# A GELU-gate kernel: the first two tiles loaded and stored in two pieces each, and the last tile computed in steps of 1, 1, 2 and 4 rows

## The chip, the cores and the metric

One core of one Trainium2 chip. The metric is the device time of one execution in microseconds (us). Times are medians of a kernel's runs.

## The reference

```python
def reference(x):                       # x: (32, 512, 2048) float32
    half_dim = x.shape[-1] // 2
    x1, x2 = x[..., :half_dim], x[..., half_dim:]
    gelu_x1 = 0.5 * x1 * (1 + erf(x1 / np.sqrt(2)))
    return (gelu_x1 * x2).astype(np.float32)   # (32, 512, 1024)
```

There are 16384 rows of 8 KB in (134.2 MB) and 4 KB out (67.1 MB).

## The kernel before

A tile is 128 partitions x 8 rows: 8.39 MB in, 4.19 MB out, 16 tiles. There are two input buffers and two output buffers. SyncE issues all loads, ScalarE issues the stores of tiles 0 to 13.

```python
    R, STEP = 8, 4
    x_t = x_flat.rearrange("(n p r) d -> n p r d", p=P, r=R)
    o_t = out_flat.rearrange("(n p r) d -> n p r d", p=P, r=R)
    ... # xpool and opool, two buffers each; load(i) fills one x_tile on SyncE
    ahead = [load(0), load(1)]
    for i in range(n_tiles):
        x_tile = ahead.pop(0)
        o_tile = opool.tile([P, R, half], out.dtype, name="o_tile")
        last = i == n_tiles - 1
        for r in range(0, R, STEP):
            rows = slice(r, r + STEP)
            nc.scalar.activation(out=x_tile[:, rows, :half], in_=x_tile[:, rows, :half], func=GELU)
            nc.vector.tensor_mul(out=o_tile[:, rows, :], in0=x_tile[:, rows, :half], in1=x_tile[:, rows, half:])
            if last:
                store(nc.sync, i, o_tile, rows)
        if not last:
            store(nc.sync if i == n_tiles - 2 else nc.scalar, i, o_tile, slice(0, R))
        if i + 2 < n_tiles:
            ahead.append(load(i + 2))
```

In memory the 8 rows of one partition lie in one piece, so a whole tile moves as runs of 64 KB (load) and 32 KB (store), half a tile as runs of 32 KB and 16 KB. The trace has one packet record for each run: in the kernel before, 2048 of 64 KB for the 16 loads of 128 partitions.

## Time and profile before

| | before |
|---|---|
| time, 3 runs | 471.6 us (471.57 to 472.48) |
| span of the profiled run | 469.7 us |
| VectorE, ScalarE busy | 30%, 25% |
| DMA engines busy | 99.5% |
| bytes over the span | 429 GB/s |

A packet record has queue, size, start and duration of one run. A completion record is the 4-byte write that ends a transfer, one for each of the 16 engines (528 in the kernel before, for its 33 transfers); a transfer has landed when the last of its 16 is there. The records do not name the engine; where I speak of single engines I have chained each packet to the one that starts as it ends. That attribution is rough where several engines run close together. By these chains a completion takes a turn of its queue: on one engine of before a load packet starts at 66.59, a store's completion at 69.02 and the next load packet at 69.03, with no store packet between.

### The profile page before, as it was taken

What the parts mean: (1) busy time and instruction counts of PE and PEld (TensorE: products, weight loads), DVE (VectorE), ACT (ScalarE), POOL (GpSimd) and SP (SyncE); (2) the same over time, 40 slices, a digit from 0 to 9 for tenths busy, and PEclk for the clock granted to TensorE, in tenths of its full rate; (3) what the DMA queues carried; (4) which work ended last, traced back from release to release, by engine and by line L of the source; (5) the groups of instructions that cost most, each with busy time, mean ns of one, the idle gap of its engine ahead of it and who ended that gap; (6) DMA issues with size and microseconds to landing.
All of it is one profiled execution on the core that took longest, in us unless ns stands there. A gap on an engine that the chain in (4) does not pass through costs nothing.

```text
span 469.7 us, 213 instructions
## 1 busy us (share of the span) xinstructions
DVE 140.2 (30%) x32; ACT 115.2 (25%) x33; POOL 0.2 (0%) x4
## 2 busy tenths in 40 slices
DVE  0070704307042070520606115060250702507043
ACT  1052306023060320603206041060500505005060
POOL 0000000000000000000000000000000000000000
DMA  8999999999999999999999999999999999999988
GB/s 357 446 446 357 446 446 446 402 446 458 391 446 444 433 463 402 435 413 491 402 419 430 491 402 402 446 491 402 402 446 480 413 402 444 449 446 402 474 375 357
DMA packets 4754, 201.35 MB, mean 429 GB/s; under 512 B 528, under 2 KB 528, under 8 KB 528
## 3 DMA queue, kind: packets, MB, share of 16 engines
q1 hardware_dynamic: 2736, 142.61, 70.5%
q10 hardware_dynamic: 2016, 58.72, 29.0%
q14 instruction: 2, 0.02, 0.0%
HBM read 134.22 MB, written 67.11 MB: 429 GB/s over the span
## 4 chain that ended last, share of the span: by engine, by line
DMA 77%; DVE 14%; ACT 6%; DVEq 1%; issue 0%; SPq 0%; ACTq 0%
DMA x_tile<-in_x_dram 77%; DVE o_tile L57 14%; ACT x_tile L54 6%; DVEq L93 1%; SPq L41 0%; ACTq L54 0%
## 5 line engine op out<-in xcount | busy, mean ns | idle before, releaser
L57 DVE TENSOR_TENSOR o_tile<-x_tile 128x4096 f32<-128x4096 f32 x32 | 140.2, 4422 | 321.6 <-ACT x_tile L54 321.6
L54 ACT ACTIVATE x_tile<-x_tile 128x4096 f32<-128x4096 f32 x32 | 114.0, 3608 | 340.5 <-DMA x_tile<-in_x_dram 340.5
L54 ACT ACT_TABLE_LOAD x1 | 1.3, 1283 | 0.7 <-PEq L82 0.7
L82 POOL MEMSET const-bfloat16-1.0<- 128x1 bf16 x1 | 0.1, 102 | 0.0
L82 POOL MEMSET const-uint8-127<- 128x1 uint8 x1 | 0.1, 101 | 0.0
L82 POOL MEMSET const-float32-0.0<- 128x1 f32 x1 | 0.1, 99 | 0.2 <-issue 0.2
L82 POOL MEMSET const-float32-1.0<- 128x1 f32 x1 | 0.1, 98 | 0.0
## 6 DMA issues: line engine op xcount, KB each, us to landing
out_dram<-o_tile ACTq DMA_DIRECT2D x14, 4096.0 KB, 41.8
out_dram<-o_tile SPq DMA_DIRECT2D x1, 4096.0 KB, 24.8
out_dram<-o_tile SPq DMA_DIRECT2D x2, 2048.0 KB, 6.9
x_tile<-in_x_dram SPq DMA_DIRECT2D x16, 45.5
```

The source lines that it names most:

```text
L54: nc.scalar.activation(out=x_tile[:, rows, :half], in_=x_tile[:, rows, :half], func=GELU)
L57: nc.vector.tensor_mul(out=o_tile[:, rows, :], in0=x_tile[:, rows, :half], in1=x_tile[:, rows, half:],)
L82: nc = _bacc.Bacc("TRN2", target_bir_lowering=False, num_devices=1)
L93: with _tile.TileContext(nc) as tc:
```

## The change

The intent: start computing and storing when half a tile has landed, and make the first half of the last tile ready sooner by small steps.

```diff
-    R, STEP = 8, 4
+    R = 8
 ...
-    ahead = [load(0), load(1)]
+    def load_small(i):
+        x_tile = xpool.tile([P, R, dim], x.dtype, name="x_tile")
+        for h in range(2):
+            rows = slice(4 * h, 4 * h + 4)
+            nc.sync.dma_start(out=x_tile[:, rows, :], in_=x_t[i][:, rows, :])
+        return x_tile
+
+    ahead = [load_small(0), load_small(1)]
 ...
-        for r in range(0, R, STEP):
-            rows = slice(r, r + STEP)
+        for lo, hi in ((0, 1), (1, 2), (2, 4), (4, 8)) if last else ((0, 4), (4, 8)):
+            rows = slice(lo, hi)
 ...
-            if last:
-                store(nc.sync, i, o_tile, rows)
-        if not last:
+            if (last or i < 2) and hi % 4 == 0:
+                store(nc.sync if last else nc.scalar, i, o_tile, slice(hi - 4, hi))
+        if 2 <= i < n_tiles - 1:
             store(nc.sync if i == n_tiles - 2 else nc.scalar, i, o_tile, slice(0, R))
```

## The prediction

> **What bounds the kernel now.** I read the page first, engines and DMA rows together:
>
> ```profile
> span 469.7 us, 213 instructions
> DVE 140.2 (30%) x32; ACT 115.2 (25%) x33; POOL 0.2 (0%) x4
> ...
> DMA  8999999999999999999999999999999999999988
> ...
> q1 hardware_dynamic: 2736, 142.61, 70.5%
> q10 hardware_dynamic: 2016, 58.72, 29.0%
> ```
>
> No compute engine is busy a third of the time; the DMA engines are full in every slice (9 is 90% or more) but the first and the last two. q1 is the SyncE queue (all loads, the last three stores), q10 the ScalarE queue (14 stores): 70.5 + 29.0 = 99.5% of the 16 engines' time. Then the chain of waits, two rounds of it:
>
> ```profile
> 56.85 45.55 DMA x_tile<-in_x_dram
> ...
> 102.48 3.62 ACT x_tile L54
> 106.11 0.03 issue
> 106.13 8.77 DVE o_tile L57 x2
> 114.90 0.02 issue
> 114.92 45.50 DMA x_tile<-in_x_dram
> ```
>
> It reads as a loop: load lands, GELU 3.62, two multiplies 8.77, the buffer is free, next load 45.5. But 45.5 is not what a load costs alone. A round is 114.92 - 56.85 = 58.07 us for two tiles, in which 2 x (8.39 + 4.19) = 25.17 MB move: 433 GB/s. Load 0, alone on the engines, needed 22.67 - 0.73 = 21.9 us. So the 45.5 is queueing behind other transfers: a bandwidth limit that looks like a loop. Head and tail, from the timeline:
>
> ```profile
> 0.73 56.45 SPq L41 DMA_DIRECT2D x_tile<-in_x_dram  x4
> 22.67 7.12 ACT L54 ACTIVATE x_tile<-x_tile 128x4096 f32<-128x4096 f32 x2 [20.66 <-DMA x_tile<-in_x_dram]
> 26.32 8.76 DVE L57 TENSOR_TENSOR o_tile<-x_tile 128x4096 f32<-128x4096 f32 x2 [26.32 <-ACT x_tile L54]
> 35.11 0.38 ACTq L45 DMA_DIRECT2D out_dram<-o_tile  x1
> ```
>
> ```profile
> 434.51 27.63 SPq L45 DMA_DIRECT2D out_dram<-o_tile  x3
> 449.37 7.12 ACT L54 ACTIVATE x_tile<-x_tile 128x4096 f32<-128x4096 f32 x2 [20.18 <-DMA x_tile<-in_x_dram]
> 453.02 8.76 DVE L57 TENSOR_TENSOR o_tile<-x_tile 128x4096 f32<-128x4096 f32 x2 [18.54 <-ACT x_tile L54]
> ```
>
> Loads 0 and 1 start together, so the first store, at 35.11, finds load 1 still on the engines. At the end load 15 lands at 449.3, store 14 (waiting in the same queue since 434.5) follows, and the halves of store 15 are issued at 457.45 and 461.80. In the trace's packet records the first data packet starts at 1.74 and the last ends at 468.51. Store 14 ends at about 458.3 on nearly every engine and store 15 starts at 458.31 to 458.8: in the whole tail the engines are idle some 0.2 us. The only other hole is at the passage from load 1 to store 0, where the last 64 KB packet of each engine takes 3.1 to 3.8 us in place of 2.42 (about 1.1 us).
>
> [...]The packet records agree: in the steady state an engine alternates one 64 KB load packet (2.42 us) with one 32 KB store packet (1.21 us), eight of each for a tile, 8 x 3.63 = 29.0 us, which is half a round; a completion record takes a turn of its own.[...]
>
> **The change, part by part.**
> (1) Split loads. Two 8 MB loads become four 4 MB loads, two more issues at about 0.33 us each on SyncE, behind running transfers. Rows 0-3 of tile 0 land near 0.73 + 21.9/2 + about 1 = 12.7, not 22.67. GELU to 16.3, multiply to 20.7, first half store at 20.7 (before: 35.1); the second half and load 2 follow load 0's rest: 22.6 + 3.6 + 4.4 = 30.6 (before 35.1). On a full DMA this moves bytes about and removes none: gain 0.
> (2) Split stores. The same bytes in 16 KB packets, where I see 0.61 us each for store 15: the same rate. But turns go by packets: a 64 KB load packet beside a 16 KB store packet gives loads 4/5, not 2/3, and each half store spends a turn of its own on completion. Until store 1 is out, loads run ahead of stores.
> (3) An issue order. In the instruction order of the changed kernel, ScalarE issues both half stores of tile 1 after both its GELUs, so the first waits for load 1's second half, near 51, plus 3.6: about 55 (before, store 1 at 56.85; now its second half near 59). By hand, with turns: store 0 done near 52, then load 2 is alone until store 1's packets come in near 60 (new packets come two or so behind those already taken up, as store 0 did: issued 35.11, first packet 42.25). Load 2 has then done about 4 of its 8 packets unaccompanied; from there one for one, load 3 ends with some 3 packets of store 1b left. That backlog of 3 to 4 packets then persists, since the turns are one for one.
> (4) What the backlog does. The output buffer of tile i is that of tile i-2, whose store now ends about 3 x 3.63 + 2.42 + 0.3 = 13.6 us after load i, and GELU is done at +4. So from tile 3 on VectorE waits about 8 to 10 us for the store. It then ends at 13.6 + 8.8 = 22.4 after load i, and issues load i+2; load i+1 ends at 29.0. Still 6 us early, so the DMA stays full: cost 0 in the steady state.
> (5) The tail. The last load lands about 4 us earlier (445 for 449), because stores are behind by 3.5 packets x 1.21. Step sizes 1, 1, 2, 4: multiplies of 1024, 1024, 2048 and 4096 take[...] 1.22 + 1.22 + 2.29 + 4.42 = 9.15 us, against 8.84: two instructions more cost 0.3. Without a buffer wait the first half would be done at +6.3 after landing (GELUs of about 1.05, 1.05 and 1.9 us, an estimate from 3.61/4 and 3.61/2 with about 0.1 added, then 2.29), not +8.1; the second at 7.6 + 4.4 = +12.0, not +12.4. Gain on the path at most the 0.2 us hole. With the buffer wait the first multiply starts only when store 13 has landed: 3 x 2.42 + 1.21 + 0.3 = 8.8 after load 15; the first half is ready at 8.8 + 4.7 = 13.5 and moves from 14.4 (0.86 us from issue to first packet, as for store 15). Store 14 has by then 3 or 4 packets done and ends at about 3 x 2.42 + 5 x 1.21 = 13.3. A hole of 1.1 us, against 0.2 now.
> Sum: 0 + 0 + 0 + (1.1 - 0.2) = +0.9 us; 471.6 + 0.9 = 472.5, and I put the middle at 472.4.
>
> **The rivals.**
> A. No backlog: if transfers go in order of issue (the first half store waiting for all of load 1), the steady state is that of before, the tail hole closes: -0.2, 471.4. Store 0's delay from 35.11 to 42.25 could be read so; the strict alternation afterwards, with the completion taking its turn, speaks for turns and a short lookahead.
> B. The intended gain: a compute-bound tail, 1.8 us sooner for the first half, 0.4 for the second, and an earlier head: 469.5 to 471. Against it: the tail holds 8.39 MB after load 15, 8.39/0.433 = 19.4 us, and 449.3 + 19.4 = 468.7 is where the data ended. It could only come from the 1.1 us hole at the first store closing.
> C. A larger backlog, 4.5 packets: the next load is issued barely in time and the tail hole grows to some 2.4 us: 473.8. More such 1.1 us holes at each first store would land there too.
>
> **Range and chances.** [...]2% slower (481) would need 9 us of idle DMA, four times rival C. From A and B below and C above, with before's runs themselves at 471.57 to 472.48: 470.7 to 474.0. Faster 0.01, same 0.98, slower 0.01.
>
> **What would show it.** Right, if VectorE waits from tile 3 on are put down to the stores and no longer to the GELU, stores of 4 MB take longer to land than 41.8 us (near 48) and loads less than 45.5 (near 37), the last GELU starts at about 445, and data ends at 469 or a little over. Rival A: waits as before, last GELU at 449. Rival B: data ending before 467.5. The sum is wrong in kind if the DMA row shows a slice under 8 in the middle.

The sum: +0.9 us, 472.5. What is cut from step 5 is only how I came to the lengths of the small steps, which the trace of before does not have. The trace of the changed kernel has them: multiplies of 128x1024, 128x2048 and 128x4096 take 1222, 2285 and 4422 ns, GELUs 1048, 1893 and 3609. The four multiplies add up to 9.15 us, but from first start to last end they take 8.90, where the two of before take 8.76. In "halves of tile 0", below, which has these tail steps and no wait on a store, the halves of the last tile are done 6.1 and 11.8 us after its first GELU starts, in before 8.1 and 12.4. An estimate from the trace: at the 433 GB/s of the round above, 201.33 MB take 465.0 us, and 2% faster would be 462.2.

## More of the kernel before

The prediction shows the page's engine and DMA rows, the chain and both ends of the timeline. Two views it does not show matter later. First what VectorE waited for (columns: us in total, times, longest us):

```profile
DVE o_tile L57 <- ACT x_tile L54: 321.6, 16, 26.3
```

VectorE waits for the GELU and never for a store. Then the DMA issues (last column: median us from issue to landing):

```profile
out_dram<-o_tile ACTq DMA_DIRECT2D x14, 4096.0 KB, 41.8
...
x_tile<-in_x_dram SPq DMA_DIRECT2D x16, 45.5
```

## The result, and the profile after

475.75 us (475.08 to 479.37, 6 runs) against 471.54 (471.3 to 472.48, 6 runs): 4.2 us slower. The ratio is 1.0101, 95% interval 1.0069 to 1.0132. Ratios here are the mean time of one kernel's runs over that of the other's runs of the same rounds, so not quite the ratio of the medians. The runs of the changed kernel also scatter over 4.3 us; five of the six runs of before lie within 0.3 us.

The page of the changed kernel:

```profile
span 473.8 us, 223 instructions
...
DMA  8999999999999999999999999999999999999987
...
q1 hardware_dynamic: 3024, 142.61, 70.0%
q10 hardware_dynamic: 2304, 58.72, 28.7%
```

The DMA engines look as full as before, in every slice but the last. That row is a mean of 16 engines over 11.8 us, and what went wrong hides in it. What VectorE waited for:

```profile
DVE o_tile L65 <- DMA out_dram<-o_tile: 178.5, 9, 20.3
DVE o_tile L65 <- ACT x_tile L62: 145.1, 9, 21.2
```

In 9 tiles VectorE's wait is now ended by a store that has to free the output buffer. The 178.5 us are the whole idle time before those tiles, not what the stores add: that is the start of the multiply less the end of its GELU step, 2.6 us at tile 4, 0.4 at tile 10, 0.1 from tile 11 to 14 and 1.9 in the last tile. The DMA issues:

```profile
out_dram<-o_tile ACTq DMA_DIRECT2D x12, 4096.0 KB, 49.0
...
out_dram<-o_tile ACTq DMA_DIRECT2D x4, 2048.0 KB, 28.1
...
x_tile<-in_x_dram SPq DMA_DIRECT2D x14, 44.8
```

A whole-tile store lands after 49.0 us, not 41.8. Both are signs of the predicted lag of stores behind loads. The loads do not: 44.8, where I expected near 37. The timeline shows why, in three places (columns: start us, us, what, count, and in brackets the idle time before it and what ended that):

```profile
20.91 0.37 ACTq L46 DMA_DIRECT2D out_dram<-o_tile  x1
...
30.60 84.26 SPq L42 DMA_DIRECT2D x_tile<-in_x_dram  x4
...
51.71 8.46 ACTq L46 DMA_DIRECT2D out_dram<-o_tile  x2
...
128.55 7.12 ACT L62 ACTIVATE x_tile<-x_tile 128x4096 f32<-128x4096 f32 x2 [21.29 <-DMA x_tile<-in_x_dram]
134.72 8.76 DVE L65 TENSOR_TENSOR o_tile<-x_tile 128x4096 f32<-128x4096 f32 x2 [20.21 <-DMA out_dram<-o_tile]
...
334.40 7.12 ACT L62 ACTIVATE x_tile<-x_tile 128x4096 f32<-128x4096 f32 x2 [22.58 <-DMA x_tile<-in_x_dram]
...
452.23 7.31 ACT L62 ACTIVATE x_tile<-x_tile 128x1024 f32<-128x1024 f32 x4 [21.88 <-DMA x_tile<-in_x_dram]
455.17 8.90 DVE L65 TENSOR_TENSOR o_tile<-x_tile 128x1024 f32<-128x1024 f32 x4 [19.43 <-DMA out_dram<-o_tile]
```

The head is nearly as predicted: half stores issued at 20.9 and 30.6, load 2 at 30.6. Tile 1's first half store waits only until its second GELU has started (51.70) and is issued at 51.71, not at 55. At tile 4 the loads are ahead, GELU at 128.55 where before it starts at 131.71. By tile 11 the lead is gone (334.40; before, 334.52). The last GELU starts 2.9 us later than before (452.23, before 449.37), not 4 earlier. And the last multiplies wait for store 13 until 455.17.

The lead melted on a few engines only. Completions of load 15, in us: before, first 448.3, middle 448.5, last 448.9. After, first 445.5, middle 445.8, last 451.8. So most engines did finish 3 us sooner (the prediction said 4); the slowest came 6 us behind them. The gap between first and last completion grew from load to load: 1.5 us at load 4 (126.6 to 128.1), 3.2 at load 9 (271.6 to 274.8), 6.3 at load 15. Between 105 and 445 us the packet records of before hold one packet that takes over 0.05 us too long; those of the changed kernel hold 61, all of them 64 KB load packets, with 13.0 us too much in sum. By my chains of packets they sit on some five engines, once or twice a tile, 0.1 to 0.6 us each; the engine that came last had some 4 us more of it than before.

The tail by stretches (columns: stretch, length, busy time of VectorE, ScalarE and GpSimd, PE clock, DMA share, GB/s), before and after:

```profile
450.00:457.40 7.40, 4.38 (x2) 6.50 (x2) 0.00 (x0) 1.00 1.00 431
457.40:458.60 1.20, 1.20 (x2) 0.00 (x0) 0.00 (x0) 1.00 0.55 232
```

```profile
450.00:457.00 7.00, 1.83 (x2) 4.77 (x4) 0.00 (x0) 1.00 1.03 445
457.00:460.60 3.60, 3.60 (x3) 2.54 (x1) 0.00 (x0) 1.00 0.25 107
```

Bytes are booked by packet and the stretches are short, so these shares are rough; but the hole is plain: from about 457.8 to 460.5 most engines have nothing to do, because store 14 is out and the first half of tile 15 is not ready. By packet records the hole is 2.1 us on the mean of the engines, before 0.2. Completions of the very last store: before 468.1 to 468.5 on all 16; after, 470.4 to 470.6 on 14 engines and 471.9 and 472.4 on two. So of the 3.9 us by which the last data ends later (468.5 to 472.4), the hole accounts for about 2 and the late engines, the stragglers, for the rest.

The hole too comes of late engines. The last multiplies wait for store 13, which the middle engine finished at 450.6 and the last one at 454.2. Twelve of the 16 were done by 451.1. Had the others come with them, the multiplies could have started near 452, the half tile been ready 4.5 us later (its three multiplies run from 455.17 to 459.7) and its store moved 0.86 us after that (in before issued at 457.45, first packet at 458.31), at about 457.4, before the engines ran dry at 457.8: no hole. That is an estimate from these trace times, not a run.

### The profile page after: what moved, and what is told of

Its sections match the earlier page's. It is cut to its first block, busy times and chain, and to the rows that moved or that the text cites. A ratio compares the mean times of both kernels' runs of the same rounds, so it can differ in the third digit from the quotient of the medians.

```text
span 473.8 us, 223 instructions
## 1 busy us (share of the span) xinstructions
DVE 140.5 (30%) x34; ACT 115.7 (24%) x35; POOL 0.2 (0%) x4
## 4 chain that ended last, share of the span: by engine, by line
DMA 82%; DVE 13%; DVEq 1%; ACT 1%; issue 0%; SPq 0%
DMA out_dram<-o_tile 72%; DVE o_tile L65 13%; DMA x_tile<-in_x_dram 10%; DVEq L101 1%; ACT x_tile L62 1%; SPq L52 0%; DVEq L65 0%
## 5 line engine op out<-in xcount | busy, mean ns | idle before, releaser
L65 DVE TENSOR_TENSOR o_tile<-x_tile 128x4096 f32<-128x4096 f32 (+2 forms) x34 | 140.5, 4171 | 323.6 <-DMA out_dram<-o_tile 178.5
L62 ACT ACTIVATE x_tile<-x_tile 128x4096 f32<-128x4096 f32 (+2 forms) x34 | 114.4, 3408 | 343.2 <-DMA x_tile<-in_x_dram 343.2
## 6 DMA issues: line engine op xcount, KB each, us to landing
x_tile<-in_x_dram SPq DMA_DIRECT2D x14, 44.8
```

## The experiments

Eighteen kernels ran, all correct. The first four undo the change part by part, the next ones copy one suspected effect into the kernel before, the last ones cut the guilty part finer. Diffs are against the kernel named. "Slow packets" are those more than 0.05 us over the usual 2.42 (64 KB), 1.21 (32 KB) or 0.61 us (16 KB), between 105 and 445 us, a copy's own packets included where a run has copies; hole means idle engine time between the last load and the last store, on the mean of 16 engines. The waits are counted as the profile puts them down: tiles in which it names a store as what ended VectorE's wait. It can name the GELU where a store ended it, as "all lag stores" will show.

| run | time, us | before | waits of VectorE on stores | slow packets, us in sum | load 15: first / last completion | hole, us |
|---|---|---|---|---|---|---|
| changed kernel | 475.75 | 471.54 | 9 | 13.0 | 445.5 / 451.8 | 2.1 |
| loads only | 471.65 | 471.55 | 0 | 0.2 | 448.1 / 449.1 | 0.5 |
| stores only | 475.5 (its four fast runs) | 471.55 | (2) | (209) | (460.3 / 464.2) | (1.5) |
| tail only | 471.61 | 471.55 | 0 | 0.2 | 448.1 / 448.9 | 0.0 |
| head only | 476.41 | 471.55 | 9 | 9.4 | 445.5 / 451.3 | 2.3 |
| half shift of loads | 471.72 | 471.65 | 0 | 0.4 | 448.3 / 449.6 | 0.6 |
| all shift of loads | 472.04 | 471.65 | 0 | 0.3 | 448.4 / 449.1 | 0.2 |
| all lag stores | 472.67 | 471.65 | 2 (by the records 10) | 12.5 | 446.7 / 448.8 | 0.8 |
| half lag stores | 471.86 | 471.65 | 7 | 0.9 | 446.0 / 448.7 | 0.0 |
| half shift, fraction | 474.15 | 471.49 | 0 | 17.9 | 449.7 / 451.9 | 1.6 |
| half lag, fraction | 473.42 | 471.49 | 9 | 19.0 | 447.4 / 449.7 | 0.2 |
| matched halves | 472.06 | 471.49 | 0 | 7.0 | 448.3 / 450.0 | 0.1 |
| half turn offset | 472.94 | 471.61 | 0 | 4.6 | 448.7 / 450.3 | 0.8 |
| two small, control | 472.11 | 471.61 | 0 | 0.5 | 448.2 / 448.9 | 0.3 |
| lag in step | 481.32 | 471.61 | 1 | 129 | 453.1 / 458.8 | 2.0 |
| issue order | 476.02 | 471.61 | 10 | 5.1 | 445.5 / 450.6 | 1.5 |
| halves of tile 0 | 471.38 | 471.47 | 0 | 0.3 | 447.9 / 448.5 | 0.0 |
| halves of tile 1 | 474.88 | 471.47 | 7 | 5.5 | 445.7 / 453.1 | 3.3 |
| lag in mid-run | 474.16 | 471.47 | 1 | 8.7 | 448.5 / 451.8 | 2.3 |

The profiled run of "stores only" counts as slow (over 1.5% above the fastest of its kernel; its granted clock is 1.000 as in all runs here), so its values stand in brackets and nothing is built on them.

### Part by part

Loads only: the kernel before with `load_small` for tiles 0 and 1.

```diff
-    ahead = [load(0), load(1)]
+    ahead = [load_small(0), load_small(1)]
```

> Only the loads of tiles 0 and 1 are split; stores and tail as before. Theory (half stores of 16 KB packets lose their turns, stores fall behind, and engines drift apart): no half stores, so VectorE waits on the GELU only, the 4 MB stores land in about 42 us as before, all 16 engines stay within 1 us: 471.5 +- 0.7 us. Rival (split loads are what sets the engines out of step): 474 or more.

471.65 us, ratio 1.0001 (0.9989 to 1.0013). No waits on stores; the stores even land sooner (33.3 us). Split loads are harmless.

Stores only: the kernel before with the change's store lines.

```diff
-            if last:
-                store(nc.sync, i, o_tile, rows)
-        if not last:
+            if (last or i < 2) and hi % 4 == 0:
+                store(nc.sync if last else nc.scalar, i, o_tile, slice(hi - 4, hi))
+        if 2 <= i < n_tiles - 1:
```

> Only the stores of tiles 0 and 1 are split; loads and tail as before. Theory: the backlog appears, and larger than in the changed kernel because store 1's halves wait longer: VectorE waits on stores in most tiles, 4 MB stores land in 48 us or more, time 474 to 477. Rival (split loads): 471.5.

476.65 us over all six runs (475.43 to 486.64), two of them slow; the four fast ones have 475.43 to 477.73 and a ratio of 1.0093 (1.0073 to 1.0113). The half stores alone bring a loss as large as the changed kernel's.

Tail only: the kernel before with the change's steps in the last tile.

```diff
-        for r in range(0, R, STEP):
-            rows = slice(r, r + STEP)
+        for lo, hi in ((0, 1), (1, 2), (2, 4), (4, 8)) if last else ((0, 4), (4, 8)):
+            rows = slice(lo, hi)
 ...
-            if last:
-                store(nc.sync, i, o_tile, rows)
+            if last and hi % 4 == 0:
+                store(nc.sync, i, o_tile, slice(hi - 4, hi))
```

> Only the 1, 1, 2, 4 steps of the last tile. Theory: the first half store is issued 1.8 us earlier after the last load, the last one 0.4 us; it closes the 0.2 us hole: 471.3, within 0.5 us of before. Rival (the smaller steps cost at the end): 472.5 or more. Rival (compute-bound tail): 470 or less.

471.61 us, ratio 1.0002 (0.9988 to 1.0015). The hole of 0.2 us closes in its records and the time does not show it.

Head only: the changed kernel with the tail as before.

```diff
-        for lo, hi in ((0, 1), (1, 2), (2, 4), (4, 8)) if last else ((0, 4), (4, 8)):
+        for lo, hi in ((0, 4), (4, 8)):
```

> Split loads and stores in the head, the tail in steps of 4 as before. Theory: all of the loss is made in the head and the time is the changed kernel's, 475 to 476. Rival (tail): 471.5 to 472.5.

476.41 us, ratio 1.0105 (1.0087 to 1.0123): as the changed kernel, with 9 waits on stores and the same spread of completions.

What was open now was how half stores of two tiles cost 4 us at the other end of the run.

### Are engines that run out of step slow?

In the changed kernel four engines take up the first half store one load packet sooner than the rest (near 24.5 us instead of 26.1) and are out of step from then on. The next four runs put that, or the lag, into the kernel before by tiny copies from output tile 4 to a scratch tile. A copy of 8 partitions has 8 packets and 8 completions (half shift of loads: 4770 packets, 536 of them under 512 B, against 4754 and 528), so it runs on 8 engines only, where I count a turn for its data and one for its completion.

```diff
+        if i == 4:
+            for k in range(1):                                   # N copies
+                s_tile = spool.tile([8, 512], x.dtype, name=f"s_tile{k}")      # PARTS, WORDS
+                nc.sync.dma_start(out=s_tile, in_=o_tile[:8, 0, :512])          # QUEUE
         if not last:
             store(nc.sync if i == n_tiles - 2 else nc.scalar, i, o_tile, slice(0, R))
```

Half shift of loads: as shown, on SyncE.

> Before plus one 16 KB copy (8 partitions, output tile 4 to a scratch tile) on the SyncE queue: on 8 of the 16 DMA engines it takes two turns of the load queue, so these 8 run out of step with the other 8 from tile 4 on, with no backlog of stores. Theory D (engines out of step make load packets slow): 473.5 or more, 8 engines with stalls. Rival B (the backlog of stores makes them slow): 471.6 to 472, no stalls.

471.72 us, ratio 1.0000 (0.9988 to 1.0012). The engines are out of step in the packet records and slow packets do not come.

All shift of loads, the control: the same with 16 partitions.

```diff
-                s_tile = spool.tile([8, 512], ...);  in_=o_tile[:8, 0, :512]
+                s_tile = spool.tile([16, 512], ...); in_=o_tile[:16, 0, :512]
```

> Control: the same copy with 16 partitions, so all 16 engines lose the same two turns and stay in step. Both theories: 471.6 +- 0.5.

472.04 us, ratio 1.0011 (0.9999 to 1.0024).

All lag stores: two copies of 16 partitions on ScalarE.

```diff
-            for k in range(1):  ... [8, 512]  ... nc.sync.dma_start
+            for k in range(2):  ... [16, 512] ... nc.scalar.dma_start
```

> Before plus two 32 KB copies (16 partitions, output tile 4 to scratch) on the ScalarE queue ahead of store 4: every engine loses four turns of the store queue, about 14 us of lag of stores behind loads, in step and without any half store. VectorE should wait on stores from tile 6 on. Theory D: only the tail hole that the prediction worked out, 472.3 to 473. Rival B: 474.5 or more, with slow load packets.

472.67 us, ratio 1.0021 (1.0009 to 1.0033), in the range of theory D and below the rival's 474.5. All engines stop for about 0.7 us at the copies themselves, in two packets each, which is nearly all of the 12.5 us of slow packets (12.5 / 16 = 0.8). The profile puts only two of VectorE's waits down to stores. Its timeline from 210 to 262 us, at tile 7, shows that this count misleads:

```profile
216.96 7.12 ACT L56 ACTIVATE x_tile<-x_tile 128x4096 f32<-128x4096 f32 x2 [21.86 <-DMA x_tile<-in_x_dram]
224.26 8.76 DVE L59 TENSOR_TENSOR o_tile<-x_tile 128x4096 f32<-128x4096 f32 x2 [20.19 <-ACT x_tile L56]
```

The first GELU step ends at 220.57, and the multiply starts 3.7 us after it. In these 3.7 us store 5, which has to free the buffer, gets its last completion (223.66). The profile names the second GELU step, which happens to end at 224.08. In every tile from 6 to 14 the multiply starts 0.5 to 0.6 us after the last completion of the store two tiles back and 3.6 or 3.7 us after its GELU step; at tile 12 VectorE passed its wait at 369.40, before the second GELU step ended (369.51). So this is the lag that was asked for, on all engines and in step. It holds VectorE up longer than the changed kernel does (at most 2.6 us), only two slow packets follow the copies, and the price is 1.0 us (by the interval 0.4 to 1.6), of which the stop at the copies can be some 0.7.

Half lag stores: two copies of 8 partitions on ScalarE.

```diff
-            for k in range(1):  ... nc.sync.dma_start
+            for k in range(2):  ... nc.scalar.dma_start
```

> The same two copies with 8 partitions, so 8 engines lag by four turns of the store queue and 8 do not. Theory D: 475 or more, the changed kernel's loss or worse. Rival B: about that of the run in which all engines lag, since a store lands when its last engine is done.

471.86 us, ratio 1.0004 (0.9992 to 1.0016), against 475 or more that the theory wanted. Its waits of VectorE:

```profile
DVE o_tile L59 <- ACT x_tile L56: 179.1, 9, 26.2
DVE o_tile L59 <- DMA out_dram<-o_tile: 142.3, 7, 20.7
```

Here are nearly as many waits on stores as in the changed kernel (7 against 9, 4 MB stores at 49.1 us), on engines in two groups apart, and the 0.2 us that it costs are within the noise. But these waits are short: beyond the GELU step the store adds 0.2 to 0.9 us a tile. So it is the run before this one that shows long waits on stores to be cheap, and this one that being out of step by whole packets costs nothing measurable. My theory, that engines out of step have slow packets, fell.

### Out of step by a fraction?

The next guess: in the changed kernel the lagging engines' packets start 1.4 to 1.8 us off the others', a fraction of a 3.63 us turn. The copies' times in the next expectations are estimates from the 2.42 us of a 64 KB packet: 12 KB 0.45, 14 KB 0.53; the 1.4 us of the control below is 4 x 1.21 and 0.15 for 4 KB, less 3.63.

Half shift, fraction: the SyncE copy of 8 partitions with 14 KB a partition.

```diff
-                s_tile = spool.tile([8, 512], ...);  in_=o_tile[:8, 0, :512]
+                s_tile = spool.tile([8, 3584], ...); in_=o_tile[:8] as 8 x 8192, first 3584 words
```

> As the neutral run with one small copy on the SyncE queue for 8 engines, but the copy has 14 KB a partition (about 0.5 us on those engines), so the two groups of engines are apart by a fraction of a packet turn and not by whole packets. Theory P (engines apart by a fraction of a turn have slow load packets, as in the changed kernel, where the lagging engines' packets start 1.4 to 1.8 us off the others'): slow packets of 0.1 to 0.6 us on one group, 472.5 or more. If P is wrong: 471.7, as with the small copy.

474.15 us, ratio 1.0055 (1.0042 to 1.0069). It looked like a hit until I read the packet records: most of the excess is one event at 161 us: while the copy runs, seven load packets take 1.0 to 1.1 us too long, eleven store packets 0.2 to 0.7 and the copy's own packets up to 0.6. After it slow packets are few (at most 0.4 us a tile in sum from 190 us on).

Half lag, fraction: as the half lag, with 2 KB and then 12 KB a partition.

```diff
-            for k in range(2): ... [8, 512] ...
+            sizes 512 and 3072 words, 8 partitions, nc.scalar
```

> As the neutral run with two small copies on the ScalarE queue for 8 engines, but the second has 12 KB a partition (0.45 us): the lag of stores and the waits of VectorE as there, plus the fraction. Theory P: slow packets, 473.5 to 476. If P is wrong: 471.9.

473.42 us, ratio 1.0040 (1.0027 to 1.0052). The same: one event at about 161 us (19.0 / 16 = 1.2 us), then one slow packet only, with 9 waits put down to stores (the store adds 0.6 to 1.3 us a tile). These two runs measure mostly a stall at such a copy, and give the guess no support.

Matched halves: the changed kernel with tiles 2 to 4 loaded in halves as well, so that 16 KB store packets meet 32 KB load packets.

```diff
-            ahead.append(load(i + 2))
+            ahead.append(load_small(i + 2) if i < 3 else load(i + 2))
```

> The changed kernel with the loads of tiles 2, 3 and 4 split in halves too, so that 16 KB store packets meet 32 KB load packets and stores keep a third of the bytes. If turns by packet make the lag: VectorE has no or few waits on stores and 4 MB stores land within 42 us; the lag's 1.0 us goes. Whether slow packets stay is open: without them 471.6, with them 472.5 to 475.

472.06 us, ratio 1.0016 (1.0003 to 1.0028). Its waits:

```profile
DVE o_tile L65 <- ACT x_tile L62: 321.2, 23, 21.9
```

No wait on a store is left, stores land in 33.0 us, and 3.6 us of the 4.2 are back, with every half store of the change in place. So by these runs a half store does little harm by itself (0.6 us here); it did where it met 64 KB load packets (4.2 us). Both the lag and the late engines went at once, so this run does not tell which of the two made the loss; "all lag stores" has the lag alone, for about 1.0 us.

Half turn offset, and its control: two small loads from HBM on SyncE for 8 engines after tile 4, with 2 KB and 12 KB a partition, and with 2 KB both times.

```diff
+        if i == 4:      # after the load of tile 6; 8 partitions of tile 0's input into scratch tiles
+            nc.sync.dma_start(out=s_tile0, in_=...[:, :512])
+            nc.sync.dma_start(out=s_tile1, in_=...[:, :3072])     # control: [:, :512]
```

> Before plus two small loads from HBM on the SyncE queue for 8 of the 16 engines, 2 KB and 12 KB a partition: four turns of the load queue and about 0.52 us, so one group of engines is 4 x 1.21 + 0.52 = 5.4 us, that is 1.7 us modulo a turn of 3.63, off the other. Theory P' (an offset of about half a turn makes load packets slow): slow packets in every tile on one group and 473 or more. If P' is wrong: 471.6 to 472.2.

> Control: both loads 2 KB a partition, offset 1.4 us or a little less: P' says fewer or no slow packets, 471.6 to 472.5; without P' 471.6 to 472.

472.94 (1.0027; 1.0015 to 1.0039) and 472.11 us (1.0009; 0.9997 to 1.0021). The first has 4.6 us of slow packets, most of it within two tiles of the copy, then none, though the groups stay apart. Its copies also hold 8 engines for about 0.5 us. The guess is not confirmed, and a later run speaks against it (halves of tile 0, below).

### The lag, by other means

Lag in step: the stores of tiles 3, 4 and 5 as two transfers of 64 partitions each, with the issue order on ScalarE pinned.

```diff
-        if not last:
-            store(nc.sync if i == n_tiles - 2 else nc.scalar, i, o_tile, slice(0, R))
+        if i in (3, 4, 5):
+            for ps in (slice(0, 64), slice(64, 128)):
+                prev = nc.scalar.dma_start(out=o_t[i][ps], in_=o_tile[ps])   # next GELU issued after it
+        elif ...
```

> Before with the stores of tiles 3, 4 and 5 each issued as two transfers of 64 partitions (same 32 KB packets, one more turn of the store queue each, all engines alike), issue order on ScalarE kept: stores lag three turns, 10.9 us, more than before. If the prediction's steps 4 and 5 hold: VectorE waits on stores from tile 6 or so on, and the time is 472.0 to 472.8. If the lag by itself brings the slow packets: 474 or more. If the lag costs nothing: 471.6.

481.32 us, ratio 1.0210 (1.0197 to 1.0223), outside every expectation. Slow packets begin near 130 us, as the first split store (issued at 115.18) reaches the engines and before a lag can be there, and the engines scatter. The way of splitting does harm of its own, with packet sizes unchanged, so the run says nothing on the lag, and mixed packet sizes are not the only way to scatter the engines. It does show that once engines have scattered, slow packets go on to the end (some 9 us in sum for each tile near 400 us), long after all transfers are ordinary again.

Issue order: the changed kernel, tile 1's first half store pinned ahead of its second GELU.

```diff
-            nc.scalar.activation(...)
+            with tc.issue_after(prev.ins) if prev else nullcontext():   # prev: ScalarE's latest store
+                nc.scalar.activation(...)
```

> The changed kernel with the first half store of tile 1 issued right after its multiply (near 45 us, not 55): the lag is about one turn less, VectorE's waits on stores shorter by some 3.6 us each or gone. If the lag sets the loss: 472 to 473. If the slow packets do, and they come with the half stores: 474 to 476.

476.02 us (473.8 to 477.64), ratio 1.0096 (1.0072 to 1.0121): no better, with 10 waits on stores. The half store is now issued at 45.34 instead of 51.71, and at tile 4 the store adds 1.9 us instead of 2.6. So the order that the prediction's step 3 blamed makes a small part of the lag and, as far as these runs show, none of the loss. The edit also holds each later GELU until ScalarE's latest store is issued.

### Which half stores

Halves of tile 0: the changed kernel, tile 1 stored whole.

```diff
-            if (last or i < 2) and hi % 4 == 0:
+            if (last or i < 1) and hi % 4 == 0:
 ...
-        if 2 <= i < n_tiles - 1:
+        if 1 <= i < n_tiles - 1:
```

> The changed kernel, but tile 1 stored whole. Tile 0's half stores meet 32 KB load packets, 2 to 1 as in the steady state, so no lag: VectorE waits on stores in at most one or two tiles, 471.6 to 472.3. If half stores do the harm whatever they meet: 474 or more.

471.38 us, ratio 0.9996 (0.9984 to 1.0008). Its waits and stores:

```profile
DVE o_tile L65 <- ACT x_tile L62: 320.1, 20, 20.9
```

```profile
out_dram<-o_tile ACTq DMA_DIRECT2D x13, 4096.0 KB, 33.1
```

No lag, hardly a slow packet (0.3 us), no loss, with everything else of the change in place. By chains, two of its engines run about 1.9 us off the rest to the end, without slow packets: being half a turn apart is not enough.

Halves of tile 1: the changed kernel, tile 0 stored whole.

```diff
-            if (last or i < 2) and hi % 4 == 0:
+            if (last or i == 1) and hi % 4 == 0:
 ...
-        if 2 <= i < n_tiles - 1:
+        if i != 1 and not last:
```

> The changed kernel, but tile 0 stored whole. Tile 1's half stores meet 64 KB load packets, 4 to 1: the lag and the waits on stores are there, 473.5 to 477. If only the early first half store (near 21 us) knocks the engines out of step: 471.6 to 472.8.

474.88 us (471.64 to 476.85, six runs), ratio 1.0060 (1.0036 to 1.0084). Lag, stragglers and hole are back. The completions of the last store: 471.3 to 471.5 on 15 engines, 473.8 on one. Of the change's four half stores in the head, it is the two of tile 1, which meet 64 KB load packets, that do the harm. How much of it comes differs from run to run: the fastest of these six, 471.64, lost 0.2 us. The loss is 3.4 us here and 4.2 in the changed kernel; with both scattering as they do, this does not show that tile 0's halves add to it.

Lag in mid-run: the kernel before with store 4 alone in two halves.

```diff
+        if i == 4:
+            store(nc.scalar, i, o_tile, slice(0, 4))
+            store(nc.scalar, i, o_tile, slice(4, 8))
-        if not last:
+        elif not last:
```

> Before with store 4 alone in two halves of 16 KB packets: nine turns more in the store queue, which the buffers cap, so the lag is at its limit from tile 6 on, with engines in step before. If being knocked out of step at the head is the cause: VectorE waits on stores, few slow packets, 472.3 to 474. If the lag itself brings slow packets: they come on most engines from tile 6 on, 475 or more.

474.16 us (474.08 to 474.32), ratio 1.0056 (1.0044 to 1.0068), between the two ranges. The lasting lag did not come: a store holds VectorE up once, for 17.7 us at tile 6, and never again. Nearly all slow packets are over by 250 us (8.7 us in sum, 0.5 us an engine). The tail, by timeline and by stretches:

```profile
452.18 7.12 ACT L54 ACTIVATE x_tile<-x_tile 128x4096 f32<-128x4096 f32 x2 [21.89 <-DMA x_tile<-in_x_dram]
455.83 8.76 DVE L57 TENSOR_TENSOR o_tile<-x_tile 128x4096 f32<-128x4096 f32 x2 [20.25 <-ACT x_tile L54]
```

```profile
458.00:461.40 3.40, 3.40 (x2) 1.31 (x1) 0.00 (x0) 1.00 0.24 101
```

One engine brings load 15 at 451.8, the middle one at 449.0; the GELU starts 2.8 us later than before, and the engines stand idle for 2.3 us in the mean before the last halves come. All 16 engines then end at 471.0 to 471.2, 2.7 us later than before. This is a hole made by one late engine, with no store that holds VectorE up and no stragglers at the end.

No version beat both kernels; the best, with halves of tile 0 only, equals the kernel before.

## Why the prediction was wrong

It said 472.4 us, 470.7 to 474.0. Measured: 475.75. Step by step:

1. **Split loads gain nothing on full engines.** Right. Loads only: 471.65 against 471.55. The predicted head times hold as well: first GELU 12.80 (12.7 predicted), first half store 20.91 (20.7), load 2 at 30.60 (30.6).
2. **Turns go by packets, so 16 KB stores beside 64 KB loads fall behind.** Right: between 60 and 100 us 224 store packets of 16 KB run beside 208 load packets of 64 KB (3.7 and 13.6 MB). The loss goes with that meeting. Matched packet sizes take the lag away (472.06); the halves of tile 0, which meet 32 KB loads, are harmless (471.38); those of tile 1 are not (474.88).
3. **The issue order adds to the lag.** The order is read rightly, but the first half store goes out at 51.71, not about 55, and the order does not matter for the loss: pinned the other way, 476.02. The backlog of 3 to 4 packets that this step counts by hand was too large, by about a factor of two: store 2 ends 6.1 us after load 4 (134.2, 128.1), not 13.6.
4. **From tile 3 on VectorE waits 8 to 10 us more for stores, and the steady state costs 0.** The waits came, in tiles 3 to 10 and in the last by the profile. They are shorter than I worked out: the multiply of tile 4 starts at 134.72, 2.6 us after its GELU step is done at 132.2, not 8 to 10. The 49.0 us of the 4 MB stores (near 48 predicted) hide this: the stores land sooner than worked out, but are also issued sooner (store 4 at 143.52, 15.4 us after load 4, not 22.4). The waits are cheap, as predicted: 3.7 us in every tile from 6 on, with all engines in step, come with a loss of 1.0, and part of that is the stop at the copies (all lag stores). But "the DMA stays full: cost 0 in the steady state" is the first step that failed. Full is not fast: 61 load packets on a few engines took 13.0 us too long in sum, and the lead of the loads melted from 3 us to nothing by tile 11.
5. **The last load lands at 445, a hole of 1.1 us in place of 0.2, sum +0.9.** This term was mis-sized, and the sum with it, because I treated the 16 engines as one. The middle engine finished load 15 at 445.8, about as predicted; the last came at 451.8, and the tile landed with its last engine (GELU at 452.23). Store 13, which I put 8.8 us after load 15, ended 4.8 after it on the middle engine (450.6) and at 454.2 on the last. So the multiplies started at 455.17, near the 445 + 8.8 = 454 that was meant, but not for the reason that I gave: the lag was about half of what I worked out, and a late engine made up the rest. That this start came out near is luck. The hole measured 2.1 us. It moves the end of 14 engines by 2.2 us (468.3 to 470.5). The stragglers end 1.9 us after these, and the end of the program is theirs: 2.2 + 1.9 = 4.1, the difference of the spans (473.8 - 469.7), against the 0.9 of the sum.
6. **The tail steps gain at most 0.2 us.** Right: 471.61 against 471.55.

Of the rivals, A (no lag) and B (the intended gain) fell. C had the size of the hole (2.4 us), but by a larger backlog, where the backlog was smaller and late engines made the hole.

One reading in the prediction needs a word. The 1.1 us at the passage from load 1 to store 0 is not "the only other hole": the first packet of load 0 also takes 2.7 to 3.6 us on each engine in place of 2.42.

What is shown by runs: with tile 0 stored whole, tile 1's two half stores still bring most of the loss (474.88 against 475.75); it is gone where tile 1 is stored whole (471.38), and nearly gone where its halves meet 32 KB load packets (472.06, 0.6 left). A lag of all engines in step costs about 1.0, the stop at the copies included. What the traces show: the loss is lost in two places, the hole near 458 us and the engines that end last, and in both the late engines are the last to come. That without them there would be no loss is argued from these times; no run removed the late engines and kept the rest. What stays open is why a few engines' 64 KB load packets take 0.1 to 0.6 us longer, tile after tile. Being out of step is not enough (half shift, halves of tile 0), a lag of the stores is not enough (all lag stores, half lag), and a half store in mid-run leaves one late engine and no lasting slow packets. Of the kernels with a fast profile, only those where tile 1's half stores meet 64 KB loads (and the one with stores by 64 partitions) have them to the end.

## What to carry to other kernels

Here, with the DMA engines full (99.5%), split loads at the head gained nothing (471.65 against 471.55), and the smaller piece had a smaller run (a half store 16 KB in place of 32): before splitting one stream, work out its packet size against that of the stream it takes turns with, and try keeping their ratio, as the runs with little or no loss did (471.38, 472.06). Keeping it is no guarantee: the split by 64 partitions kept it and lost 9.7 us. Read a full DMA row as a mean of 16 engines; look at first and last completion of a transfer, because here the slowest engine ended it (load 15: first 445.5, last 451.8, GELU at 452.23). Check a wait that the profile names against the times: the whole idle gap goes to the releaser that came last, and it can name the wrong one ("all lag stores", tile 7: it names the GELU step that ended at 224.08, not store 5, which landed at 223.66). And a gain at one end of the program must be followed to the other: this kernel's first 60 us set how its last 20 went.
